# Sliding-window attention in halves of the TensorE array, with the softmax scaled on ScalarE

## The chip, the cores and the metric

The kernel runs on one core of one Trainium2 chip. The metric is the device time of one execution in microseconds (us). A core has TensorE (PE in the tables; PEld is its loading of weights), VectorE (DVE), ScalarE (ACT), GpSimd (POOL), and SyncE (SP), which issues most transfers. Each engine works through its own instructions in order; semaphores tie them together.

## The reference, cut to what matters

One decoder block on 256 tokens with model width 2048. Two attention branches run side by side and are merged by sigmoid gates; then follow an output projection, two RMSNorms and a gated feed-forward network with a short convolution. The change touches the attention of both branches:

```python
# MLA branch: 16 heads, query and key of 128 + 64, value of 128, causal
s = (einsum('bqhd,bkhd->bhqk', qn, k_nope) + einsum('bqhd,bkd->bhqk', qr, k_rope)) * scale
s = where(kpos[None, :] <= qpos[:, None], s, NEG)
p = softmax(s); o = einsum('bhqk,bkhd->bqhd', p, v)
# sliding branch: 32 heads of 64, 4 key/value heads, window 128, T5 bias, one sink per head
s = where(mask, einsum('bnqhgd,bnshd->bhgnqs', q, kb) * 0.125 + bias, NEG)
m = maximum(max(s), sink); e = exp(s - m)
p = e / (sum(e) + exp(sink - m)); o = einsum('bhgnqs,bnshd->bnqhgd', p, vb)
```

Everything is float32. The large products are made in three passes: each operand is split into a high part in the reduced format fp32r and a remainder in the same format, and high*high, high*low and low*high are summed.

## The kernel before, in words

The 1.5 ms are mostly weights that stream in, are split (`whi` by ScalarE on L116, `wlo` by VectorE on L117) and multiplied on TensorE (L129 to L131 and L137 to L139). The attention lies in the middle, from about 330 to 695 us. It is a loop over 8 pairs `i` (L593). In a pair, `pair_proj` makes the next pair's queries, keys and values; `step(2 * i)` and `step(2 * i + 1)` do the attention; `late_z` and, towards the end, the output projection give TensorE other matmuls. While they run, a background generator adds up modulation rows on VectorE (L235). A scheduler of the framework, working from its own estimates, sets the order of each engine's instructions at build time, so matmuls of the projections stand between those of the attention.

One `step(h)` handles one MLA head (index 0) and two sliding heads (1 and 2). Each has 256 queries as two blocks of 128; the first block sees 128 keys, the second 256, so a score matrix is 128 x 384. Its parts are:

- Scores (L520 to L530). Each head takes one PSUM bank of tag `sc`, of which there are two. For a sliding head the 64-row query is stacked: `stack` (L442 to L450) writes its high part into one half of the 128 rows and its remainder into the other half, and the keys `kss` hold the same 64 rows twice. One 128-row matmul thus gives high*k + low*k; two of them, for the keys' high and low part, make a block (L530).
- Mask, bias and row maximum on VectorE (L535), which frees the bank; then -max (L538), the sink (L540), exponentials with sums on ScalarE (L546) and 0.5/sum on VectorE (L548 to L550).
- Normalisation, six multiplications per step: `NORMS = "dpdpda"` gives the three 128-wide ones to VectorE, two 256-wide ones to GpSimd (both L558), and the last 256-wide one to ScalarE (L556).
- Three transposes per head on TensorE into a bank `tp` (L143 through L561), copied by ScalarE to `pT` (L563).
- Value products (L570, L571) into bank `o`: first the MLA head, with 128 output rows, then each sliding head with 64 output rows, head 1 in the lower and head 2 in the upper half. These operands are plain float32, and each such matmul shows up as two records in the trace.
- Gating (L573) and merging into `mix` (L576).

## Time and profile before

| | before |
|---|---|
| time, median of 3 runs | 1520.65 us (1518.46 to 1521.5) |
| time of the profiled execution | 1520.17 us |
| its span | 1518.3 us |
| PE busy | 1472.3 us (97%) |
| DVE busy | 1050.1 us (69%) |
| ACT busy | 754.4 us (50%) |
| POOL busy | 286.9 us (19%) |

The span runs from the first to the last instruction; some 2 us of the profiled time lie around it. A busy share is an average over stages, and the end of a matmul record is modelled: consecutive matmuls overlap, so what a matmul costs is read from the distance between starts, not from its duration.

### The profile page before, as it was taken

What the parts mean: (1) busy time and instruction counts of PE and PEld (TensorE: products, weight loads), DVE (VectorE), ACT (ScalarE), POOL (GpSimd) and SP (SyncE); (2) the same over time, 40 slices, a digit from 0 to 9 for tenths busy, and PEclk for the clock granted to TensorE, in tenths of its full rate; (3) what the DMA queues carried; (4) which work ended last, traced back from release to release, by engine and by line L of the source; (5) the groups of instructions that cost most, each with busy time, mean ns of one, the idle gap of its engine ahead of it and who ended that gap; (6) DMA issues with size and microseconds to landing.
All of it is one profiled execution on the core that took longest, in us unless ns stands there. A gap on an engine that the chain in (4) does not pass through costs nothing.

```text
span 1518.3 us, 27322 instructions
## 1 busy us (share of the span) xinstructions
PE 1472.3 (97%) x10914; PEld 1361.0 (90%) x10914; DVE 1050.1 (69%) x1384; ACT 754.4 (50%) x1165; POOL 286.9 (19%) x207
## 2 busy tenths in 40 slices
PE   7999999799999999999899999999999999999998
PEld 6988899789898898978799999999999999888886
DVE  3578868888787969777787777765666665444443
ACT  4534435545654655765564444554554454444342
POOL 0034215832525444320000010000000000000000
PEclk9999999999999999999999999999999999999999
DMA  9889868589587968669477788755556557666662
GB/s 371 295 313 328 308 234 262 178 264 306 175 306 240 298 197 274 197 208 358 183 250 259 254 277 266 225 181 183 182 181 190 182 181 242 191 193 192 194 193 99
DMA packets 101535, 357.14 MB, mean 235 GB/s; under 512 B 11760, under 2 KB 12208, under 8 KB 100896
## 3 DMA queue, kind: packets, MB, share of 16 engines
q1 hardware_dynamic: 99936, 350.82, 69.4%
q0 software_dynamic: 1472, 4.58, 1.2%
q8 instruction: 85, 1.39, 0.4%
q14 instruction: 42, 0.34, 0.1%
HBM read 351.11 MB, written 4.24 MB: 234 GB/s over the span
## 4 chain that ended last, share of the span: by engine, by line
PE 79%; DVE 9%; DMA 7%; issue 3%; ACT 1%; POOL 0%; DVEq 0%; SPq 0%; ACTq 0%; POOLq 0%
PE bk_mm L129 12%; PE bk_mm L131 12%; PE bk_mm L130 12%; PE bk_mm L137 4%; PE bk_mm L138 4%; PE bk_mm L139 4%; DMA raw<-in_w_ada_dram 4%; PE bk_sc L130 4%; PE bk_sc L129 4%; PE bk_sc L131 4%; PE bk_sc L138 3%; PE bk_sc L137 3%; PE bk_sc L139 3%; DVE wlo L117 3%; DVE acc L235 3%
## 5 line engine op out<-in xcount | busy, mean ns | idle before, releaser
L117 DVE TENSOR_TENSOR wlo<-raw,whi 128x1024 fp32r<-128x1024 f32 (+3 forms) x472 | 589.7, 1256 | 317.2 <-ACT whi L116 316.0
L116 ACT CAST whi<-raw 128x1024 fp32r<-128x1024 f32 (+3 forms) x472 | 478.1, 1019 | 531.7 <-PE bk_mm L130 161.6
L129 PE MATMUL bk_mm<-h_hi,whi 128*128 128x256 f32 x1824 | 522.6, 287 | 0.8 <-ACT h_hi L151 0.5
L131 PE MATMUL bk_mm<-h_hi,wlo 128*128 128x256 f32 x1824 | 518.0, 284 | 0.5 <-DVE wlo L117 0.5
L130 PE MATMUL bk_mm<-h_lo,whi 128*128 128x256 f32 x1824 | 518.4, 284 | 0.1
L129 PEld LDWEIGHTS bk_mm<-h_hi,whi 128*128 128x128 f32 x1824 | 350.9, 192 | 14.2 <-issue 8.7
L130 PEld LDWEIGHTS bk_mm<-h_lo,whi 128*128 128x128 f32 x1824 | 351.2, 193 | 1.1 <-issue 0.8
L131 PEld LDWEIGHTS bk_mm<-h_hi,wlo 128*128 128x128 f32 x1824 | 351.2, 193 | 1.2 <-DVE wlo L117 0.7
L235 DVE SCALAR_TENSOR_TENSOR acc<-raw,csil,acc 128x1024 f32<-128x1024 f32 (+1 forms) x141 | 188.6, 1337 | 58.2 <-DMA raw<-in_w_ada_dram 58.0
L129 PE MATMUL bk_sc<-h_hi,whi 128*128 128x256 f32 x560 | 158.7, 283 | 0.0
L130 PE MATMUL bk_sc<-h_lo,whi 128*128 128x256 f32 x560 | 158.6, 283 | 0.0
L131 PE MATMUL bk_sc<-h_hi,wlo 128*128 128x256 f32 x560 | 158.5, 283 | 0.0
L746 POOL TENSOR_TENSOR sa<-sa,u 128x512 f32<-128x512 f32 x22 | 32.7, 1486 | 469.1 <-DVE u L740 447.6
L129 PEld LDWEIGHTS bk_sc<-h_hi,whi 128*128 128x128 f32 x560 | 107.5, 192 | 0.4 <-ACT whi L116 0.4
L130 PEld LDWEIGHTS bk_sc<-h_lo,whi 128*128 128x128 f32 x560 | 107.5, 192 | 0.2 <-DVE h_lo L152 0.2
L131 PEld LDWEIGHTS bk_sc<-h_hi,wlo 128*128 128x128 f32 x560 | 107.5, 192 | 0.0
L363 POOL TENSOR_TENSOR pair<-pair,part 128x512 f32<-128x512 f32 x35 | 64.0, 1830 | 195.2 <-ACT part L362 195.1
L137 PE MATMUL bk_sc<-whi,g_hi 128*128 128x512 f32 x176 | 68.6, 390 | 0.0
L137 PE MATMUL bk_mm<-whi,g_hi 128*128 128x512 f32 x176 | 68.6, 390 | 0.0
L138 PE MATMUL bk_mm<-wlo,g_hi 128*128 128x512 f32 x176 | 68.5, 389 | 0.0
L139 PE MATMUL bk_mm<-whi,g_lo 128*128 128x512 f32 x176 | 68.5, 389 | 0.0
L138 PE MATMUL bk_sc<-wlo,g_hi 128*128 128x512 f32 x176 | 68.5, 389 | 0.0
(202 smaller groups left out, 2102.8 us busy)
## 6 DMA issues: line engine op xcount, KB each, us to landing
raw<-in_w_ada_dram SPq DMA_DIRECT2D x192, 512.0 KB, 5.0
raw<-in_w_up_dram SPq DMA_DIRECT2D x176, 512.0 KB, 4.3
raw<-in_w_in_dram SPq DMA_DIRECT2D x116, 512.0 KB, 5.1
raw<-in_w_down_dram SPq DMA_DIRECT2D x88, 512.0 KB, 4.4
raw<-in_w_o_dram SPq DMA_DIRECT2D x32, 512.0 KB, 5.0
raw<-in_w_uqn_dram SPq DMA_DIRECT2D x16, 384.0 KB, 4.1
bias<-trow POOLq DMA_DIRECT2D x16, 256.0 KB, 5.2
raw<-in_w_ukv_dram SPq DMA_DIRECT2D x16, 256.0 KB, 3.5
```

The source lines that it names most:

```text
L116: act.copy(hi[:, :n], raw[:, :n])
L117: dve.tensor_tensor(lo[:, :n], raw[:, :n], hi[:, :n].bitcast(F32), op=ALU.subtract)
L129: pe.matmul(o, wh, xh, start=start, stop=False)
L130: pe.matmul(o, wh, xl, start=False, stop=False)
L131: pe.matmul(o, wl, xh, start=False, stop=stop)
L137: pe.matmul(o, ch, wh, start=start, stop=False)
L138: pe.matmul(o, ch, wl, start=False, stop=False)
L139: pe.matmul(o, cl, wh, start=False, stop=stop)
L235: dve.scalar_tensor_tensor(acc[:, :w], r, csil[:, j:j + 1], acc[:, :w], op0=ALU.mult, op1=ALU.add)
L363: pool.tensor_tensor(pairs[i][:, :wd], pairs[i][:, :wd], part[:, :wd], op=ALU.add)
L746: pool.tensor_tensor(sa, sa, us[1], op=ALU.mult)
```

## The change

Three edits inside `step`, with a helper. First, the sliding heads' queries are no longer stacked: `split_pair2` keeps both heads in one tile, head 1 in rows 0 to 63 and head 2 in rows 64 to 127, with a tile for the high parts (`qsh`) and one for the remainders (`qsl`). The scores are 64-row matmuls, three per block and head (high*high, high*low, low*high), written head 1, head 2, head 1, ... so that neighbours use different row halves of the array and different banks. The sliding heads now come ahead of the MLA head. Second, all six normalisations go to ScalarE and `NORMS` disappears. Third, the value products come after all three heads' transposes, with three `pT` buffers in place of two: the two sliding heads alternate between the column halves, and the MLA head follows.

```diff
--- before.py
+++ after.py
@@ -30,7 +30,6 @@
 PUMP = 1.3
 RATES = (0.5, 0.8, 0.3, 0.5)
 SPREAD = 7.0
-NORMS = "dpdpda"
 SCT = (2, 4)
 NW1 = (5, 5, 5)
 NW2 = (4, 6, 6)
@@ -449,6 +448,14 @@
             pool.tensor_tensor(res[e][other], src[me], res[e][me].bitcast(F32), op=ALU.subtract)
         return res
 
+    def split_pair2(src):
+
+        hi = at.tile([P, 2 * T], F32R, tag="qsh", bufs=1, name="qsh")
+        lo = at.tile([P, 2 * T], F32R, tag="qsl", bufs=1, name="qsl")
+        act.copy(hi, src)
+        pool.tensor_tensor(lo, src, hi.bitcast(F32), op=ALU.subtract)
+        return hi, lo
+
     MLA_SCALE = 192.0 ** -0.5
     mixs = [None] * 8
     mx2 = []
@@ -505,8 +512,8 @@
         e = h % 2
         kv = h // 4
         if e == 0:
-            stacks[h // 2] = (stack(ropes[h // 2], "qr", T), stack(zt[h // 2][0], "qs", 2 * T))
-        qrs, qss = stacks[h // 2]
+            stacks[h // 2] = (stack(ropes[h // 2], "qr", T), split_pair2(zt[h // 2][0]))
+        qrs, qs = stacks[h // 2]
         zp = zt[h // 2]
         vst = pairs[7]
         bias = at.tile([P, 2, T], F32, tag="bias", name="bias")
@@ -517,30 +524,41 @@
 
         sm = at.tile([P, 3, 384], F32, tag="sm", bufs=2, name="sm")
         mx = at.tile([P, 6], F32, tag="mx", name="mx")
-        for i in range(3):
-            sc = bank("sc")
-            for c0, c1, q0, kw in ((0, P, 0, P), (P, 384, P, T)):
-                qsl = slice(e * T + q0, e * T + q0 + P)
-                if i == 0:
-                    pe.matmul(sc[:, c0:c1], qn[:, qsl], kn[:, e * T:e * T + kw], start=True, stop=False)
-                    for j in range(2):
-                        pe.matmul(sc[:, c0:c1], qrs[e][:, q0:q0 + P], krs[:, j, :kw], start=False, stop=j == 1)
-                else:
-                    for j in range(2):
-                        pe.matmul(sc[:, c0:c1], qss[i - 1][:, qsl], kss[:, j, kv, T - kw:], start=j == 0, stop=j == 1)
+        blocks = ((0, P, 0, P), (P, 384, P, T))
+
+        def masked(i, sc):
             for j, (c0, c1) in enumerate(((0, P), (P, 384))):
                 col = 2 * i + j
                 bt = cmask[:, P - c0:T] if i == 0 else bias[:, i - 1, :c1 - c0]
                 to = sm[:, i, c0:c1]
-                dve.tensor_tensor_reduce(to if i == 0 else down_order(to), sc[:, c0:c1], bt, 1.0, sink6[:, h, col:col + 1],
+                dve.tensor_tensor_reduce(to if i == 0 else down_order(to), sc[:, c0:c1], bt, 1.0,
+                                         sink6[:, h, col:col + 1],
                                          op0=ALU.add, op1=ALU.max, accum_out=mx[:, col:col + 1])
+
+
+        scs = [bank("sc") for _ in range(2)]
+        for c0, c1, q0, kw in blocks:
+            qsl = slice(e * T + q0, e * T + q0 + P)
+            for n, (qp, kp) in enumerate(((0, 0), (0, 1), (1, 0))):
+                for i in range(2):
+                    r = slice(64 * i, 64 * i + 64)
+                    pe.matmul(scs[i][:, c0:c1], qs[qp][r, qsl], kss[r, kp, kv, T - kw:], start=n == 0, stop=n == 2)
+        for i in range(2):
+            masked(i + 1, scs[i])
+        sc = bank("sc")
+        for c0, c1, q0, kw in blocks:
+            qsl = slice(e * T + q0, e * T + q0 + P)
+            pe.matmul(sc[:, c0:c1], qn[:, qsl], kn[:, e * T:e * T + kw], start=True, stop=False)
+            for j in range(2):
+                pe.matmul(sc[:, c0:c1], qrs[e][:, q0:q0 + P], krs[:, j, :kw], start=False, stop=j == 1)
+        masked(0, sc)
         nm = at.tile([P, 6], F32, tag="nm", name="nm")
         dve.tensor_scalar(nm, mx, -1.0, None, op0=ALU.mult)
         es = at.tile([P, 6], F32, tag="es", name="es")
         dve.tensor_tensor(es, sink6[:, h, :], nm, op=ALU.add)
         act.activation(es, es, AF.Exp)
         den = at.tile([P, 6], F32, tag="den", name="den")
-        for i in range(3):
+        for i in (1, 2, 0):
             for j, (c0, c1) in enumerate(((0, P), (P, 384))):
                 col = 2 * i + j
                 act.activation(sm[:, i, c0:c1], sm[:, i, c0:c1], AF.Exp, bias=nm[:, col:col + 1],
@@ -549,26 +567,23 @@
         dve.reciprocal(den, den)
         dve.tensor_scalar(den, den, 0.5, None, op0=ALU.mult)
         ob = bank("o")
-        for i in range(3):
+        pts = [None] * 3
+        for i in (1, 2, 0):
+            tp = bank("tp")
             for j, (c0, c1) in enumerate(((0, P), (P, 384))):
-                o, r = sm[:, i, c0:c1], den[:, 2 * i + j:2 * i + j + 1]
-                if NORMS[2 * i + j] == "a":
-                    act.mul(o, o, r)
-                else:
-                    (dve if NORMS[2 * i + j] == "d" else pool).tensor_scalar(o, o, r, None, op0=ALU.mult)
-            tp = bank("tp")
+                act.mul(sm[:, i, c0:c1], sm[:, i, c0:c1], den[:, 2 * i + j:2 * i + j + 1])
             for c in range(3):
                 turn_pe(tp[:, c * P:c * P + P], sm[:, i, c * P:c * P + P])
-            pT = at.tile([P, 384], F32, tag="pT", bufs=2, name="pT")
-            act.copy(pT, tp[:, :384])
-            if i == 0:
-                o = ob[:, 0:T]
-                vv = [vt[:, t * T + e * P:t * T + e * P + P] for t in range(2)]
-            else:
-                o = ob[64 * (i - 1):64 * i, T:2 * T]
-                vv = [vst[:, t * T + kv * 64:t * T + kv * 64 + 64] for t in range(2)]
-            pe.matmul(o, vv[0], pT[:, 0:T], start=True, stop=False)
-            pe.matmul(o[:, P:T], vv[1], pT[:, T:384], start=False, stop=True)
+            pts[i] = at.tile([P, 384], F32, tag="pT", bufs=3, name="pT")
+            act.copy(pts[i], tp[:, :384])
+
+        for t in range(2):
+            for i in (1, 2):
+                pe.matmul(ob[64 * (i - 1):64 * i, T + t * P:2 * T], vst[:, t * T + kv * 64:t * T + kv * 64 + 64],
+                          pts[i][:, t * T:T + t * P], start=t == 0, stop=t == 1)
+        for t in range(2):
+            pe.matmul(ob[:, t * P:T], vt[:, t * T + e * P:t * T + e * P + P], pts[0][:, t * T:T + t * P],
+                      start=t == 0, stop=t == 1)
         tm = at.tile([P, 512], F32, tag="tmp", name="tm")
         dve.scalar_tensor_tensor(tm, tg, 1.0, ob, op0=ALU.add, op1=ALU.mult)
         if e == 0:
```

The instructions move as follows; names carry buffer numbers, `bk_sc` is a score bank, `bk_o` the output bank, `bk_mm` and `bk_tp` the banks of other products and of transposes. Lines of the changed kernel are shifted: L545 are its sliding scores, L551 and L553 the MLA scores, L582 the sliding value products, L585 the MLA ones, L574 the normalisation, and L128 to L130, L142, L239 and L115 are L129 to L131, L143, L240 and L116 of before.

TensorE before, scores at the border of the third and fourth step:

```order
L530 MATMUL bk_sc_4519<-kss_2760,qs_4493 128x128 x2
L530 MATMUL bk_sc_4519<-kss_2760,qs_4493 128x256 x2
L525 MATMUL bk_sc_4581<-kn_3811,qn_3769 128x128
L527 MATMUL bk_sc_4581<-krs_2759,qr_4487 128x128 x2
L525 MATMUL bk_sc_4581<-kn_3811,qn_3769 128x256
L527 MATMUL bk_sc_4581<-krs_2759,qr_4487 128x256 x2
L129 MATMUL bk_mm_4653<-h_hi_243,whi_4656 128x256
```

TensorE of the changed kernel, sliding scores of the third step, the first of a pair (banks 4507 and 4508 are the two heads):

```order
L138 MATMUL bk_mm_4465<-whi_4458,blk_lo_3178 128x256
L545 MATMUL bk_sc_4507<-kss_2760,qsh_4498 128x128
L545 MATMUL bk_sc_4508<-kss_2760,qsh_4498 128x128
L545 MATMUL bk_sc_4507<-kss_2760,qsh_4498 128x128
L545 MATMUL bk_sc_4508<-kss_2760,qsh_4498 128x128
L545 MATMUL bk_sc_4507<-kss_2760,qsl_4499 128x128
L545 MATMUL bk_sc_4508<-kss_2760,qsl_4499 128x128
L545 MATMUL bk_sc_4507<-kss_2760,qsh_4498 128x256
L545 MATMUL bk_sc_4508<-kss_2760,qsh_4498 128x256
L545 MATMUL bk_sc_4507<-kss_2760,qsh_4498 128x256
L545 MATMUL bk_sc_4508<-kss_2760,qsh_4498 128x256
L545 MATMUL bk_sc_4507<-kss_2760,qsl_4499 128x256
```

And of the fourth step, the second of its pair, whose head 1 stands 25 projection matmuls earlier:

```order
L128 MATMUL bk_mm_4665<-h_hi_633,whi_4734 128x256
L545 MATMUL bk_sc_4590<-kss_2760,qsh_4498 128x128 x2
L545 MATMUL bk_sc_4590<-kss_2760,qsl_4499 128x128
L545 MATMUL bk_sc_4590<-kss_2760,qsh_4498 128x256 x2
L545 MATMUL bk_sc_4590<-kss_2760,qsl_4499 128x256
L551 MATMUL bk_sc_4607<-kn_3811,qn_3769 128x128
L553 MATMUL bk_sc_4607<-krs_2759,qr_4493 128x128 x2
L551 MATMUL bk_sc_4607<-kn_3811,qn_3769 128x256
L553 MATMUL bk_sc_4607<-krs_2759,qr_4493 128x256 x2
```

In the first step of a pair the heads alternate as written; in the second step the scheduler has taken them apart, and one head's six matmuls stand alone between other work.

TensorE, value products of the fourth step, before and then changed:

```order
L131 MATMUL bk_mm_4785<-h_hi_2574,wlo_4808 128x256
L570 MATMUL bk_o_4619<-pT_4626,vt_3854 128x256
L571 MATMUL bk_o_4619<-pT_4626,vt_3854 128x128
L570 MATMUL bk_o_4619<-pT_4636,pair_426 64x256
L571 MATMUL bk_o_4619<-pT_4636,pair_426 64x128
L240 MATMUL bk_tp_4792<-acc_3827,ones_87 32x256 x4
L129 MATMUL bk_mm_4785<-h_hi_2580,whi_4807 128x256
```

```order
L128 MATMUL bk_mm_4797<-h_hi_2580,whi_4886 128x256
L582 MATMUL bk_o_4631<-pT_4638,pair_426 64x256
L582 MATMUL bk_o_4631<-pT_4646,pair_426 64x256
L582 MATMUL bk_o_4631<-pT_4638,pair_426 64x128
L582 MATMUL bk_o_4631<-pT_4646,pair_426 64x128
L585 MATMUL bk_o_4631<-pT_4654,vt_3854 128x256
L585 MATMUL bk_o_4631<-pT_4654,vt_3854 128x128
L239 MATMUL bk_tp_4804<-acc_3827,ones_87 32x256 x4
```

Before, head 2's products follow later and by themselves; now both sliding heads stand together, ahead of the MLA head.

ScalarE around the normalisation of the first two steps, before and then changed:

```order
L541 ACTIVATE es<-es 128x6
L556 ACTIVATE sm<-sm,den 128x256
L116 CAST whi<-raw 128x768
L563 COPY pT<-bk_tp 128x384
L116 CAST whi<-raw 128x512
L563 COPY pT<-bk_tp 128x384
L556 ACTIVATE sm<-sm,den 128x256
L116 CAST whi<-raw 128x512
L563 COPY pT<-bk_tp 128x384 x2
```

```order
L574 ACTIVATE sm<-sm,den 128x256
L574 ACTIVATE sm<-sm,den 128x128
L574 ACTIVATE sm<-sm,den 128x256
L574 ACTIVATE sm<-sm,den 128x128
L574 ACTIVATE sm<-sm,den 128x256
L115 CAST whi<-raw 128x768
L578 COPY pT<-bk_tp 128x384
L115 CAST whi<-raw 128x768
L578 COPY pT<-bk_tp 128x384
```

Before, two multiplications stand among casts and copies; now twelve stand in a row (the last five are shown) ahead of the first copy.

## Rows read from the trace of the kernel before

**Rows 1.** The page: busy time and share of each engine; then the chain of work that ended last, by engine.

```profile
PE 1472.3 (97%) x10914; PEld 1361.0 (90%) x10914; DVE 1050.1 (69%) x1384; ACT 754.4 (50%) x1165; POOL 286.9 (19%) x207
...
PE 79%; DVE 9%; DMA 7%; issue 3%; ACT 1%; POOL 0%; DVEq 0%; SPq 0%; ACTq 0%; POOLq 0%
```

**Rows 2.** Busy time by stretch: start and end, length, busy us and instructions of PE, PEld, DVE, ACT and POOL, granted TensorE clock, DMA share, GB/s. The first is the whole attention, the others two short stretches in it.

```profile
330.00:695.00 365.00, 351.85 (x2578) 321.52 (x2578) 292.63 (x525) 209.34 (x461) 135.10 (x105) 0.99 0.75 245
...
337.00:343.00 6.00, 5.16 (x29) 5.09 (x30) 6.00 (x15) 2.41 (x4) 0.73 (x1) 0.72 0.89 316
601.00:606.00 5.00, 4.62 (x26) 4.48 (x27) 3.76 (x11) 2.13 (x4) 2.61 (x3) 0.66 0.91 292
```

**Rows 3.** What PE waited for from 330 to 700 us: total us, times, longest us.

```profile
PE bk_sc L530 <- DVE mx L535: 7.3, 5, 2.9
PE bk_tp L143 <- DVE sm L558: 5.0, 5, 2.1
PE bk_tp L143 <- POOL sm L558: 0.7, 2, 0.4
```

**Rows 4.** Timeline of PE around one sliding head's value product: start us, length us, instruction, records (start to start is the cost).

```profile
377.04 0.28 PE L129 MATMUL bk_mm<-blk_hi,whi 128*128 128x256 f32 x1
377.16 0.28 PE L130 MATMUL bk_mm<-blk_lo,whi 128*128 128x256 f32 x1
377.37 0.65 PE L570 MATMUL bk_o<-pT,pair 128*64 128x256 f32 x2
377.85 0.38 PE L571 MATMUL bk_o<-pT,pair 128*64 128x128 f32 x2
378.16 0.39 PE L131 MATMUL bk_mm<-blk_hi,wlo 128*128 128x256 f32 x1
378.39 0.28 PE L129 MATMUL bk_mm<-blk_hi,whi 128*128 128x256 f32 x1
378.50 0.28 PE L130 MATMUL bk_mm<-blk_lo,whi 128*128 128x256 f32 x1
```

**Rows 5.** The same view of an MLA head's value product, with 128 output rows.

```profile
616.57 0.28 PE L131 MATMUL bk_mm<-blk_hi,wlo 128*128 128x256 f32 x1
616.69 0.60 PE L570 MATMUL bk_o<-pT,vt 128*128 128x256 f32 x2
617.12 0.38 PE L571 MATMUL bk_o<-pT,vt 128*128 128x128 f32 x2
```

**Rows 6.** The same view of float32 products with 32 output rows: two of them (four records) on two quarters of the columns, and four of them (eight records) on all four quarters.

```profile
112.48 0.28 PE L131 MATMUL bk_mm<-h_hi,wlo 128*128 128x256 f32 x1
112.69 0.63 PE L227 MATMUL bk_sc<-raw,cpad 128*32 128x256 f32 x4
113.25 0.39 PE L137 MATMUL bk_mm<-whi,h_hi 128*128 128x256 f32 x1
...
157.98 0.28 PE L129 MATMUL bk_mm<-h_hi,whi 128*128 128x256 f32 x1
158.19 0.64 PE L240 MATMUL bk_sc<-acc,ones 128*32 128x256 f32 x8
158.76 0.38 PE L130 MATMUL bk_mm<-h_lo,whi 128*128 128x256 f32 x1
```

**Rows 7.** The same view of one sliding head's scores: two matmuls of 128 columns and two of 256 in one row.

```profile
625.56 0.28 PE L129 MATMUL bk_mm<-h_hi,whi 128*128 128x256 f32 x1
625.68 0.63 PE L530 MATMUL bk_sc<-kss,qs 128*128 128x128 f32 x4
626.14 0.29 PE L130 MATMUL bk_mm<-h_lo,whi 128*128 128x256 f32 x1
```

**Rows 8.** The same view of the one product of the program on fewer than 128 rows: 32 rows and 32 columns of the array, 384 columns streamed.

```profile
243.33 0.28 PE L131 MATMUL bk_mm<-h_hi,wlo 128*128 128x256 f32 x1
243.54 0.83 PE L318 MATMUL bk_tp<-oh,c_rel_bias 32*32 32x384 f32 x2
244.29 0.39 PE L129 MATMUL bk_mm<-h_hi,whi 128*128 128x256 f32 x1
244.52 0.28 PE L130 MATMUL bk_mm<-h_lo,whi 128*128 128x256 f32 x1
```

**Rows 9.** Groups by line and shape from 330 to 695 us (busy us, mean ns | idle before): the normalisations, and the exponentials of the same shapes.

```profile
L558 POOL TENSOR_SCALAR sm<-sm,den 128x256 f32<-128x256 f32 x32 | 43.2, 1358 | 44.6 <-DVE den L550 44.4
...
L546 ACT ACTIVATE sm<-sm,nm 128x128 f32<-128x128 f32 x48 | 18.8, 392 | 9.8 <-DVE nm L538 9.7
...
L558 DVE TENSOR_SCALAR sm<-sm,den 128x128 f32<-128x128 f32 x48 | 16.4, 405 | 0.2
...
L556 ACT ACTIVATE sm<-sm,den 128x256 f32<-128x256 f32 x16 | 8.1, 507 | 4.7 <-DVE den L550 4.6
```

**Rows 10.** Splitting the stacked queries (L448, L449), by line: number of each shape, ns min/median/max, first and last start. Then two groups of other lines with 128 rows of 512: busy us, mean ns | idle before.

```profile
L448 ACT CAST qs<-pair x16: 603/617/621, 265.0 to 629.2; 64x512 fp32r<-64x512 f32 x16
...
L449 POOL TENSOR_TENSOR qs<-pair,qs x16: 1286/1458/2302, 273.4 to 631.9; 64x512 fp32r<-64x512 f32 x16
...
L151 ACT CAST h_hi<-mix 128x512 fp32r<-128x512 f32 x8 | 4.8, 617 | 0.0
...
L746 POOL TENSOR_TENSOR sa<-sa,u 128x512 f32<-128x512 f32 x22 | 32.7, 1486 | 469.1 <-DVE u L740 447.6
```

**Rows 11.** The longest wait of ScalarE from 260 to 700 us: total us, times, longest us.

```profile
ACT whi L116 <- DMA raw<-in_w_in_dram: 43.2, 26, 3.7
```

## The prediction

> **What bounds the kernel now.** I read the page first: TensorE is busy 97% of the span, and 79% of the chain that ended last is its work [rows 1]. Then the table by stretch: in the 365 us of the attention TensorE is busy 351.85 us, VectorE 292.6, ScalarE 209.3, GpSimd 135.1 [rows 2]. Only 13.1 us are idle, and the list of waits names them: 7.3 us for a score bank that VectorE has not emptied, 5.0 and 0.7 us for transposes whose input VectorE or GpSimd has not normalised [rows 3]. Nothing there waits for weights. So the stage is as long as TensorE's own work plus these 13.1 us, and the timeline by starts tells what each matmul costs.
>
> **What it costs to leave the full array.** Between two projection matmuls lie 0.12 us (377.04 to 377.16), but the first 64-row product starts 0.21 after its forerunner, its two 256-column records take 0.48 together, the two of 128 columns 0.31, and the second projection matmul behind comes after 0.23 [rows 4]. An MLA product of the same shape needs 0.43 for the two 256-column records [rows 5], so half of that, 0.22, for the two of 128: 0.65 of pure work. From 377.16 to 378.39 are 1.23 us; less two steps of 0.12 that would be there anyway, the excursion costs 0.99, of which 0.34 are entering and leaving the mode. Two products on different column quarters take 0.56 us start to start and four take 0.57 [rows 6]: column parts do run at the same time.
>
> **Value products.** Before, 32 excursions of 0.99: 31.7 us. After, I counted the order: in 11 of 16 steps both heads stand together, one excursion of 0.65 + 0.34 = 0.99; in five steps other matmuls come between the first head's 256-column product and the rest, two excursions with 0.43 + 0.65 of work and 2 x 0.34 of mode: 1.76. Sum 10.9 + 8.8 = 19.7, a gain of 12.0 us. If halves did not overlap, the 11 steps would lose 0.65 each and the five 0.22: 8.2 back.
>
> **Scores.** Before, a sliding head's four matmuls take 0.46 us and change no mode [rows 7]: 32 x 0.46 = 14.7 us. That is 0.23 for one of 128 and one of 256 columns, so three products of a head are 3 x 0.23 = 0.69. After, in the first step of a pair the two heads alternate; if row halves overlap like column parts, that is 0.69 for both, 8 x 0.69 = 5.5. In the second step the heads stand apart, nothing overlaps, and 8 x 2 x 0.69 = 11.0. Then the mode: 12 excursions in the first steps (three of them are cut into pieces) and 16 in the second, 28 in all. The trace has no product on row halves. The nearest row is the one on 32 rows and 32 columns: the first start is 0.21 behind its forerunner, and the matmul after next follows after 0.23, as for 64 output rows [rows 8]. So I take 0.34 again, 9.5 us, with bounds of 0 (halving rows alone might need no change) and 0.45. The sum is 26.0, a loss of 11.3 us; with the bounds of the mode, 1.8 to 14.4.
>
> So the two halves of the change nearly cancel on TensorE: -12.0 + 11.3 = -0.7, and some 0.3 more for the pairs that are cut: -0.4. The MLA scores and products, and the transposes, are as many as before.
>
> A rule of the Trainium skill speaks against this sum: its page "TensorE: Matmul & The Clock Gate", Part 3 (Packing small matmuls), says that weight loads overlap matmuls in flight only where the row group differs, and the second steps use one row group six times running. This trace contradicts the rule for full-height matmuls, which share all row groups and still start 0.12 apart; for half-height ones no row shows it, so it is a rival below. The same section gives 3.07 times for four row tiles, not 4. By that ratio the alternating steps would cost some 0.90, not 0.69, an estimate of 1.7 us more.
>
> **Normalisation.** VectorE loses 48 instructions of 405 ns (16.4 us) and GpSimd 32 of 1358 (43.2); ScalarE gains 32 more of 507 ns (16.2) and 48 of 128 columns, for which the exponential of that shape, 392 ns, is the nearest row (18.8) [rows 9]. Splitting queries gives a little back: ScalarE casts 8 times instead of 16, at 617 ns, so 4.9 less, and GpSimd subtracts 8 times instead of 16 at 1458, 11.7 less [rows 10]; a tile of 128 rows takes as long as one of 64, as the 128x512 rows of other lines show, 617 and 1486 [rows 10]. ScalarE ends 30.1 us up, at 239 of 365 us; VectorE 16.4 down, at 276. None of this is on the path by itself: what counts is who waits.
>
> The waits for score banks, 7.3 us, come from VectorE's queue, and idle TensorE then runs at a lower clock for a while: the granted clock is 0.72 in 6 us around one such wait and 0.66 in 5 us after a wait for a transpose [rows 2]. At 1.2 GHz in place of 2.4 for 0.56 of 6 us and 0.68 of 5 us, each costs 1.7 us more. VectorE gets a twentieth of its work taken off and the sliding scores come earlier, before a pair's projections are done. I let the 7.3 + 1.7 = 9.0 us halve: -4.5, with bounds of 0 and -9.0. The waits for transposes, 5.7 + 1.7 = 7.4 us, I leave as they are: ScalarE takes over from two engines, and behind a multiplication that waits for its sum stand the casts of weights and the `pT` copies, whose absence TensorE would feel next. Twelve multiplications in a row, some 5.4 us, delay the first copy; TensorE has projection matmuls in between. If that cover is too short, the stall is new; if ScalarE is never late, the 7.4 us vanish.
>
> **Sum.** The profiled execution took 1520.17 us, 1.9 more than its span and 0.5 less than the median. 1520.2 - 0.4 - 4.5 = 1515.3 on that scale, 1515.8 against the median of 1520.65.
>
> **Rivals.**
> - Row halves need no change of mode. For it: the matmul streams the same 128 output columns as the full one. Against it: the 32-row product [rows 8], which also narrows the columns and so does not decide. It gives back 9.5: 1506.3.
> - Row halves hide no weight loads (slower). Mechanism and place: in the second steps the same half is loaded and used six times in a row. Price: a start that is not covered comes 0.10 late, as the matmul at 378.39 does (0.23 for 0.12) [rows 4]; 16 excursions of six, 9.6 us, and six pairs in each of eight alternating steps, 4.8; less 1.4 already in the mode cost, 13: 1528.8. It decides from about 0.06 us per matmul on. Against it: full-height matmuls do hide theirs.
> - ScalarE becomes what TensorE waits for (slower). For it: it already waits 43.2 us for weights from memory in these stages, with its queue blocked [rows 11], and the multiplications now stand in that queue. If half of the 16 steps wait as long as the longest now, 2.1 us [rows 3], that is 16.8 instead of 5.7: 1527.
> - Halves do not overlap at all, so the change does not do what it says: 8.2 from the values and 8 x 0.69 = 5.5 from the scores: 1529.5. Rows 6 speak against it for columns.
> - VectorE's relief shortens no wait, as the banks are asked for just as soon: 1520.2.
>
> **How the numbers follow.** Forecast 0.40, no mode change 0.15, weight loads 0.12, ScalarE 0.13, no overlap 0.05, no shorter wait 0.15. The range for 8 in 10 reaches from the free mode, 1506, to the slower rivals, 1529; the forecast's own is 1510 to 1521. A measurement of this kernel tells some 0.2%, 3 us, from no change: faster is below 1517.6, slower above 1523.7. Of the forecast I count two thirds as faster and nearly all the rest as no change; the free mode as faster; the last rival mostly as no change; the three others mostly as slower. This makes 0.46 faster, 0.29 no change, 0.25 slower.
>
> **What would show it.** In the timeline: two L582 of different heads some 0.01 us apart in their first record and about 1.0 us for the pair with its mode changes; two L545 of different banks likewise, and 0.7 us between the first and the last of twelve plus 0.34. If second steps show more than 0.12 between L545 starts, weight loads are not hidden; if the first L545 follows its forerunner after 0.12, the mode is free. In the list of waits, PE for the score bank should fall to some 3.7 us, and PE on ScalarE for L142 stay near 5.7; a sum of waits above 15 us, or PE's busy time in the attention off by more than 5 us, would make the forecast wrong.

## The result and the profile after

| | before | changed |
|---|---|---|
| median, us | 1520.49 (1518.46 to 1521.5, 4 runs) | 1528.47 (1526.01 to 1530.25, 4 runs) |
| ratio, 95% interval | | 1.0054 (1.0040 to 1.0067) |
| span of the profiled execution | 1518.3 | 1525.5 |

The changed kernel is slower by 8 us, 0.5%. I had forecast 1515.8, and called a time above 1523.7 slower. The page of the changed kernel, busy time and chain by engine, beside [rows 1]:

```profile
PE 1477.5 (97%) x10978; PEld 1365.7 (90%) x10978; DVE 1031.9 (68%) x1336; ACT 773.9 (51%) x1237; POOL 236.2 (15%) x167
...
PE 79%; DMA 9%; DVE 6%; issue 3%; ACT 2%; POOL 1%; DVEq 0%; SPq 0%; ACTq 0%; POOLq 0%
```

Nothing there tells where 8 us went. The table by stretch, columns as in [rows 2], tells more: the attention before, then the attention of the changed kernel and two short stretches in it.

```profile
330.00:700.00 370.00, 356.85 (x2601) 325.66 (x2601) 294.56 (x527) 211.75 (x467) 135.10 (x105) 0.99 0.76 248
```

```profile
330.00:700.00 370.00, 354.58 (x2614) 323.44 (x2613) 273.86 (x464) 228.84 (x532) 83.41 (x65) 0.97 0.74 240
386.00:395.00 9.00, 8.20 (x49) 7.49 (x49) 6.51 (x22) 3.36 (x14) 3.57 (x3) 0.81 0.84 251
581.00:592.00 11.00, 9.54 (x41) 8.91 (x42) 11.00 (x23) 3.46 (x4) 2.68 (x3) 0.53 0.85 265
```

TensorE idles 15.4 of 370 us, and 13.2 before. GpSimd lost 52 us of work and VectorE 21, as the edit meant them to, but the granted clock is 0.97 where it was 0.99: from 581 to 592 us it is 0.53, nearly all at 1.2 GHz in place of 2.4. What PE waited for from 330 to 700 us (columns as in [rows 3]):

```profile
PE bk_sc L551 <- DVE mx L534: 11.1, 4, 4.2
PE bk_mm L136 <- ACT qn L491: 2.1, 1, 2.1
PE bk_mm L128 <- ACT whi L115: 1.0, 1, 1.0
PE bk_o L582 <- DVE tm L588: 0.7, 1, 0.7
PE bk_mm L136 <- ACT whi L115: 0.5, 1, 0.5
```

The waits of transposes for a normalised input, 5.7 us before, are gone. The waits for a score bank rose from 7.3 to 11.1, in fewer and longer pieces. One of them in the timeline, TensorE and then VectorE (start, length, instruction):

```profile
578.12 0.28 PE L130 MATMUL bk_mm<-h_hi,wlo 128*128 128x256 f32 x1
582.46 0.80 PE L551 MATMUL bk_sc<-kn,qn 128*128 128x128 f32 x2 [4.06 <-DVE mx L534]
```

```profile
576.01 2.32 DVE L234 SCALAR_TENSOR_TENSOR acc<-raw,csil,acc 128x1024 f32<-128x1024 f32 x1
578.25 2.29 DVE L116 TENSOR_TENSOR wlo<-raw,whi 128x1024 fp32r<-128x1024 f32 x1
580.46 1.27 DVE L234 SCALAR_TENSOR_TENSOR acc<-raw,csil,acc 128x1024 f32<-128x1024 f32 x1
581.66 0.34 DVE L534 CUSTOM_DVE_ANT_0 sm<-bk_sc,bias,c_sink 128x128 f32<-128x128 f32 x1
581.93 0.47 DVE L534 CUSTOM_DVE_ANT_0 sm<-bk_sc,bias,c_sink 128x256 f32<-128x256 f32 x1
```

The MLA head's scores now come third and want the bank of the first sliding head. That head's scores were written from 572.2 us on; its mask takes 0.7 us, but stands in VectorE's queue behind two `acc` and a `wlo`. TensorE stands still for 4.06 us, and the low clock of the row 581 to 592 goes with it.

**One table for all runs.** To compare kernels I cut TensorE's time from 40 us to the first `sa<-u` (785.8 us before; what the change touches lies ahead of it) into three: gaps over 0.15 us, half of the busy time in stretches at 1.2 GHz (an estimate of what the low clock cost), and the rest, work at full clock. Kernels with the very same TensorE instructions gave 705.7 to 710.6 us of work, and rows_mla comes out 6 us below what its excursions add up to, so a work figure is good to some 6 us. These three are one execution's. The last column is not: the granted clock, as a share of the full one, is known for every execution, and (1 - clock) x span, averaged over all of a kernel's (4 of the changed kernel, 114 of before), is what the low clock cost in the whole span, good to 1 or 2 us.

| kernel | median, us | ratio to before (95%) | gaps | lost to low clock | work | low clock, all executions |
|---|---|---|---|---|---|---|
| before | 1520.5 | | 26.9 | 8.3 | 710.4 | 18.1 |
| changed | 1528.5 | 1.0054 (1.0040 to 1.0067) | 27.9 | 15.8 | 706.8 | 25.2 |
| v_only | 1518.8 | 0.9988 (0.9978 to 0.9999) | 30.4 | 10.0 | 703.4 | 18.1 |
| v21 | 1512.8 | 0.9956 (0.9940 to 0.9972) | 32.5 | 11.2 | 696.2 | 17.9 |
| s_only | 1532.6 | 1.0085 (1.0070 to 1.0101) | 28.1 | 14.0 | 716.9 | 20.4 |
| first_only | 1528.7 | 1.0050 (1.0032 to 1.0068) | 34.9 | 13.9 | 708.2 | 19.6 |
| rows_mla | 1528.6 | 1.0055 (1.0033 to 1.0077) | 20.7 | 9.2 | 723.7 | 13.7 |
| n_only | 1527.9 | 1.0053 (1.0035 to 1.0071) | 30.2 | 15.7 | 706.3 | 19.8 |
| n_dve | 1523.7 | 1.0025 (1.0012 to 1.0038) | 32.7 | 12.2 | 705.7 | 19.4 |
| n_pool | 1517.3 | 0.9987 (0.9974 to 0.9999) | 30.2 | 10.6 | 708.9 | 16.9 |
| act_dup | 1520.5 | 0.9994 (0.9980 to 1.0009) | 29.8 | 7.5 | 710.6 | 14.0 |
| after_stacked | 1515.9 | 0.9977 (0.9966 to 0.9989) | 31.9 | 16.3 | 695.0 | 20.8 |
| as_split | 1514.7 | 0.9962 (0.9950 to 0.9974) | 36.4 | 13.2 | 693.6 | 21.2 |
| as_split21 | 1511.6 | 0.9951 (0.9933 to 0.9968) | 34.6 | 12.3 | 692.6 | 19.5 |
| as_21 | 1514.4 | 0.9963 (0.9949 to 0.9977) | 36.5 | 17.0 | 692.1 | 20.7 |
| after_pool | 1518.6 | 0.9991 (0.9982 to 1.0000) | 27.7 | 10.3 | 706.5 | 19.7 |
| after_mlasc | 1524.2 | 1.0025 (1.0011 to 1.0040) | 27.3 | 12.0 | 709.6 | 20.3 |
| after_3sc | 1543.9 | 1.0152 (1.0130 to 1.0174) | 50.7 | 19.4 | 702.2 | 27.4 |
| best_mla | 1511.6 | 0.9943 (0.9927 to 0.9960) | 31.9 | 12.6 | 694.0 | 20.4 |
| best_dadada | 1514.9 | 0.9966 (0.9950 to 0.9981) | 36.0 | 13.2 | 694.8 | 19.4 |

The median of before was 1519.2 to 1520.1 in the later comparisons; differences to before in the text below are the ratio's, taken times 1520. Of the changed kernel's 7.2 us of span, 4.8 arise ahead of the first `sa<-u`: work -3.6, gaps +1.0, low clock +7.5. The other 2.4 come later; a stretch at 1.2 GHz near 967 us, which before has not, is worth 1.7 of them. Three other kernels show such a stretch, and I leave its cause open. The last column agrees on what the loss is: 7.1 us more low clock in the four executions, of 8 us in all.

### The profile page after: what moved, and what is told of

It is laid out like the page before. It is cut to its first block, busy times and chain, and to the rows that moved or that the text cites. A ratio compares the mean times of both kernels' runs of the same rounds, so it can differ in the third digit from the quotient of the medians.

```text
span 1525.5 us, 27386 instructions
## 1 busy us (share of the span) xinstructions
PE 1477.5 (97%) x10978; PEld 1365.7 (90%) x10978; DVE 1031.9 (68%) x1336; ACT 773.9 (51%) x1237; POOL 236.2 (15%) x167
## 4 chain that ended last, share of the span: by engine, by line
PE 79%; DMA 9%; DVE 6%; issue 3%; ACT 2%; POOL 1%; DVEq 0%; SPq 0%; ACTq 0%; POOLq 0%
PE bk_mm L128 13%; PE bk_mm L130 12%; PE bk_mm L129 12%; DMA raw<-in_w_ada_dram 5%; PE bk_mm L136 4%; PE bk_mm L137 4%; PE bk_mm L138 4%; PE bk_sc L128 4%; PE bk_sc L129 4%; PE bk_sc L130 4%; PE bk_sc L138 3%; PE bk_sc L136 3%; PE bk_sc L137 3%; DVE wlo L116 2%; DMA raw<-in_w_in_dram 2%
## 5 line engine op out<-in xcount | busy, mean ns | idle before, releaser
L116 DVE TENSOR_TENSOR wlo<-raw,whi 128x1024 fp32r<-128x1024 f32 (+3 forms) x472 | 586.7, 1251 | 317.5 <-ACT whi L115 310.5
L115 ACT CAST whi<-raw 128x1024 fp32r<-128x1024 f32 (+3 forms) x472 | 477.4, 1019 | 518.4 <-PE bk_mm L129 148.9
L128 PE MATMUL bk_mm<-h_hi,whi 128*128 128x256 f32 x1824 | 524.8, 288 | 1.9 <-ACT whi L115 1.0
L130 PE MATMUL bk_mm<-h_hi,wlo 128*128 128x256 f32 x1824 | 519.9, 286 | 0.0
L129 PE MATMUL bk_mm<-h_lo,whi 128*128 128x256 f32 x1824 | 519.7, 285 | 0.0
L128 PEld LDWEIGHTS bk_mm<-h_hi,whi 128*128 128x128 f32 x1824 | 352.0, 193 | 16.6 <-issue 9.7
L129 PEld LDWEIGHTS bk_mm<-h_lo,whi 128*128 128x128 f32 x1824 | 352.1, 193 | 2.0 <-issue 1.6
L130 PEld LDWEIGHTS bk_mm<-h_hi,wlo 128*128 128x128 f32 x1824 | 351.8, 193 | 1.0 <-issue 0.2
L234 DVE SCALAR_TENSOR_TENSOR acc<-raw,csil,acc 128x1024 f32<-128x1024 f32 (+1 forms) x141 | 192.2, 1363 | 71.2 <-DMA raw<-in_w_ada_dram 70.8
L128 PE MATMUL bk_sc<-h_hi,whi 128*128 128x256 f32 x560 | 159.1, 284 | 0.0
L129 PE MATMUL bk_sc<-h_lo,whi 128*128 128x256 f32 x560 | 158.7, 283 | 0.0
L130 PE MATMUL bk_sc<-h_hi,wlo 128*128 128x256 f32 x560 | 158.7, 283 | 0.0
L128 PEld LDWEIGHTS bk_sc<-h_hi,whi 128*128 128x128 f32 x560 | 107.9, 193 | 0.4 <-issue 0.4
L129 PEld LDWEIGHTS bk_sc<-h_lo,whi 128*128 128x128 f32 x560 | 107.8, 192 | 0.0
L130 PEld LDWEIGHTS bk_sc<-h_hi,wlo 128*128 128x128 f32 x560 | 107.8, 192 | 0.0
L761 POOL TENSOR_TENSOR sa<-sa,u 128x512 f32<-128x512 f32 x22 | 32.5, 1479 | 472.0 <-DVE u L755 453.8
```

Source lines behind the costliest of these rows:

```text
L115: act.copy(hi[:, :n], raw[:, :n])
L116: dve.tensor_tensor(lo[:, :n], raw[:, :n], hi[:, :n].bitcast(F32), op=ALU.subtract)
L128: pe.matmul(o, wh, xh, start=start, stop=False)
L129: pe.matmul(o, wh, xl, start=False, stop=False)
L130: pe.matmul(o, wl, xh, start=False, stop=stop)
L234: dve.scalar_tensor_tensor(acc[:, :w], r, csil[:, j:j + 1], acc[:, :w], op0=ALU.mult, op1=ALU.add)
```

## The experiments

### The value products alone

```diff
+        pts = [None] * 3        # all three transposes first
...
+        for t in range(2):
+            for i in (1, 2):    # v21: (2, 1)
...
```

v_only: 

> The kernel before with one part of the change: the value products stand together after the last transpose, the two sliding heads' on column halves in turn; scores and normalisation as before. Both theories put TensorE's work 12.0 us lower (32 excursions into another mode of 0.99 us become 16 cheaper ones), so about 1508.5 us, a ratio of 0.992. Theory W (the work terms of the prediction hold, and the loss of the change came from longer waits for score banks and the slower clock behind them): the banks' order is that of before, so the waits for the masks stay near 7 us and the time falls by nearly the whole 12 us, 1507 to 1512. Theory R (the row halves cost much more than the 11.3 us I put on them, and the waits are a side show): the same here. A time above 1516 would say that the value term itself was wrong.

v21: 

> The kernel before with only its value products moved together, the second sliding head's written first; its order now cuts none of the 16 excursions, where the first such kernel, with the heads written the other way, cut 15. Work by the price list: 16 x 0.99 = 15.8 us against 31.7, so 15.9 us less. Theory B (what eats savings is the bank order with the sliding heads' scores first; here the MLA head's come first as before): waits for the masks stay near 7 us and nearly all of it shows, 1502 to 1506. Theory P (VectorE's work and the loads behind it pace this stretch too, so that work saved on TensorE mostly turns into waits and slow clock, wherever they fall): TensorE's idle time between 250 and 785 us grows from 27 us to 32 or more, 1508 to 1514.

v_only is 1.8 us faster, not 12. I had assumed that heads written together stay together; its trace shows that the scheduler put the first head's first product ahead of the second head's transposes in 15 of 16 steps, two excursions each. 15 x 1.76 + 0.99 = 27.4 us, 4.3 less than before, and TensorE's time in value products fell by 3.8 us. With the later head written first none is cut: 12.5 us less in value products, 14.2 less work. Time in value products is counted from start to start and takes in the MLA head's. The price list holds; but 15.9 us were expected and 6.7 came. Gaps grew by 5.6, as theory P has it, though the banks are asked for in the old order. The low clock, 2.9 us more in this trace, is no more than before's over all executions (17.9 and 18.1).

### The scores alone

```diff
# s_only: split_pair2, row halves and MLA scores last, as changed
# rows_mla: s_only with the MLA head's scores first
# first_only: before, with
-        for i in range(3):
+        for i in (1, 2, 0):
             sc = bank("sc")
```

s_only: 

> The kernel before with the other part: sliding heads' scores on the row halves, first, and the MLA head's behind them; value products and normalisation as before. Theory W: work 11.3 + 0.3 us up, and the two banks taken at once bring the longer waits of the changed kernel too (4 us more, with 7 us more of slow clock), so 1532 to 1544, and the waits for the masks near 11 us, not 7. Theory R (row halves alone cost about 20 us): 1540, with the waits as before, near 7 us, and no more slow clock than before.

first_only: 

> The kernel before with only the order of a step's stacked scores changed, the two sliding heads' ahead of the MLA head's: the same instructions on every engine. Theory B2 (that order alone makes the longer waits of the third bank, 10 to 13 us against 7.3): 4 us of waits and some slow clock more, 1524 to 1530. Theory O: 1514 to 1526, no sign foretold.

rows_mla: 

> The kernel before with the sliding heads' scores on row halves but the MLA head's scores left first, so without the new order of scores that cost 7.6 us by itself. Nearly every lone head's six matmuls are an excursion of their own (32 in all): 32 x 0.39 = 12.5 us by the price list. If the price list holds and order is apart: 1530 to 1534. If the 12.5 us of the run with both (rows and sliding heads first) were mostly the order's, with 7.6 of them, rows cost 4 to 6 us and this is 1523 to 1527.

s_only's 12.9 us look like the term of the prediction, but they are a mixture. first_only issues the same instructions as before and loses 7.6 us; the scheduler makes a new order of it on every engine. Its attention, and its two largest waits from 330 to 700 us, of which the first is that of the MLA scores, now third in a step:

```profile
330.00:700.00 370.00, 347.96 (x2532) 319.54 (x2531) 286.78 (x510) 207.22 (x456) 139.79 (x102) 0.97 0.72 238
```

```profile
PE bk_sc L525 <- DVE mx L535: 9.8, 4, 4.1
PE bk_mm L137 <- ACT qn L484: 3.9, 1, 3.9
```

In all, first_only waits 12.1 us for score banks there, 4.8 more than before, and its gaps in the table are 8.0 us longer. The low clock is 1.5 us more over all executions, so most of its loss is waiting.

rows_mla has the rows without that order: 13.3 us more work in the table. The 12.5 of its expectation are the mode's price alone (0.39 a head, measured below) and leave out the third matmul of a block. With it a lone head takes 0.69 + 0.39 = 1.08 us, and the list gives 32 x (1.08 - 0.46) = 19.8; in its trace most lone heads take 1.07 or 1.08 us. The time is only 8.4 us up, and the waits shrink:

```profile
330.00:700.00 370.00, 364.81 (x2632) 329.52 (x2631) 285.18 (x523) 201.93 (x447) 127.53 (x98) 0.99 0.72 238
```

```profile
PE bk_sc L553 <- DVE mx L535: 1.9, 3, 1.0
PE bk_sc L542 <- DVE mx L535: 1.7, 1, 1.7
```

The waits for score banks are 3.6 us, half of before's 7.3, which fits a TensorE that comes later for them. So each lone head costs in work what the list says, and the order of the scores costs by itself. Whether the two add is not shown: 8.4 + 7.6 is 3.1 more than s_only's 12.9, but s_only's heads overlap in part and cost some 6 us less by the list.

### The normalisation alone

```diff
-NORMS = "dpdpda"
+NORMS = "aaaaaa"      # n_only;  n_dve "apapaa";  n_pool "dadada"
...
+                if NORMS[2 * i + j] != "a":          # act_dup, NORMS as before
+                    act.mul(dup[:, c0:c1], cmask[:, P - c0:T], r)
```

n_only: 

> The kernel before with all six normalisations of a step on ScalarE and nothing else. Theory W and theory R: ScalarE is 51% busy, nothing changes beyond 2 us: 1518.5 to 1522.5. Rival S (ScalarE's added 80 to 90 instructions put off what TensorE waits for): the loss of the change is here, 1526 to 1530, with more TensorE waits released by ScalarE.

n_dve: 

> The kernel before with only VectorE's three normalisations of a step moved to ScalarE (48 of 96 in all; GpSimd keeps its two). Theory L (ScalarE's added load itself costs, by putting off casts and copies that others wait for): half to two thirds of the 8 us, 1523 to 1526. Theory O (the new order decides: each placing of the same work lands its gaps and slow stretches differently, up to some 8 us either way): no fixed relation to the 8 us, anywhere in 1516 to 1528.

n_pool: 

> The kernel before with only GpSimd's two normalisations of a step moved to ScalarE (32 in all; VectorE keeps its three). Theory L: a third of the 8 us, 1522 to 1524. If GpSimd's slow normalisations of 1.36 us were what TensorE waits for: 1516 to 1519. Theory O: anywhere in 1516 to 1528.

act_dup: 

> The kernel before with its normalisation left where it is, and ScalarE given the same 80 scalings again beside it, on a constant tile and into a tile that nothing reads (about 32 us of ScalarE). Theory L: the load alone brings the 8 us, 1526 to 1530. Theory O: the time follows the gaps; if TensorE's order of instructions stays that of before, 1518 to 1522.

n_only costs 8.1 us, as rival S said, but act_dup gives ScalarE the same load and costs nothing:

```profile
330.00:700.00 370.00, 355.30 (x2599) 323.66 (x2598) 290.70 (x527) 236.17 (x543) 138.32 (x105) 1.00 0.76 246
```

ScalarE is 236.17 us busy there, more than in the changed kernel, and the granted clock is 1.00. So, in that kernel, it isn't ScalarE's load. n_dve and n_pool, +3.8 and -2.0, differ in sign. The trace of n_only has more stretches at 1.2 GHz (15.7 us lost against 8.3), but over its six executions the low clock costs only 1.7 us more than before, so most of its loss is something else; its gaps are 3.3 us longer. Its order on every engine is a new one; which moved instruction makes the loss, these runs don't tell.

### Parts taken back from the changed kernel

```diff
# after_stacked: the changed kernel with
-        scs = [bank("sc") for _ in range(2)]
...
+        for i in (1, 2, 0):
+            sc = bank("sc")
...
# as_split: after_stacked with NORMS = "dpdpda" back; as_split21: and
-            for i in (1, 2):
+            for i in (2, 1):
# as_21: after_stacked with (2, 1);  after_pool: the changed kernel with NORMS back
```

after_stacked: 

> The changed kernel with the sliding heads' scores taken back to stacked full-row products, still ahead of the MLA head's; value products and normalisation as changed. Theory W: TensorE's work falls by 12 us from the changed kernel's, and since one bank at a time is asked for, the waits for masks fall from 11 us towards 7 and the slow stretches go from 27 us towards 14: 1507 to 1513. Theory R: 1508, all from the row halves' work, with the waits still near 11 us. The waits and the granted clock of the trace tell the two apart, not the time alone.

as_split: 

> Stacked scores with the sliding heads first and value products together, as in the run before, but the normalisation shared among the three engines as in the kernel before. Its order keeps 15 of 16 steps' sliding value products in one excursion and cuts one: 15 x 0.99 + 1.76 = 16.6 us against 31.7, so work is 15.1 us below the kernel before. Theory N (putting all normalisations on ScalarE costs about 8 us by itself, as it did alone, through more and longer gaps and slow clock behind them): that cost is gone, 1505, range 1502 to 1508, and the slow stretches of the trace near 20 us in all. Rival C (the 8 us belonged to that kernel's order by chance, and every new order pays about as much): 1513, with 30 us or more of slow stretches.

as_split21: 

> As the run before it, with the second sliding head's value product written ahead of the first's; its order cuts no excursion: 16 x 0.99 = 15.8 us, work 15.9 us below the kernel before. Theory N: 1504, range 1501 to 1508. Rival C: 1512.

after_pool: 

> The changed kernel with only the normalisation taken back to three engines; scores on row halves, value products together (15 whole excursions, 1 cut: 3.1 us less work than the changed kernel's 11 and 5). Theory N: 1528.2 - 3.1 - 8 = 1517, range 1513 to 1521. Rival C, and the theory that row halves' work is the whole loss: only the 3.1 us go, 1525.

as_21: 

> Stacked scores, normalisation all on ScalarE, value products with the second sliding head's first: its order cuts none of the 16 excursions where the same kernel with the other order cut 6, so 6 x 0.77 = 4.6 us less work than its 1515.9. Theory N: 1511, range 1508 to 1515. Rival C: anything from 1505 to 1518, set by its gaps.

Without row halves the changed kernel is 11.7 us faster and beats before by 3.5: the rows' work (11.8 less) is worth its price there. Theory W's second half fell: the waits for masks did not shrink (9.9 + 2.7 us from 330 to 700), as theory R has it. The low clock cost as much as in the changed kernel in this trace (16.3 us), but 4.4 us less over all executions. Taking the normalisation back gave the changed kernel 9.6 us (3.1 from value excursions), as theory N said; with stacked scores it gave only 2.3 (as_split, whose value excursions alone should give 3.9) and 1.8 (as_split21 against as_21), as rival C said. So the price of the normalisation isn't a constant either. In the traces of all four pairs (n_only and before, changed and after_pool, after_stacked and as_split, as_21 and as_split21) having it on ScalarE lost 3.1 to 7.4 us more to low clock, but over all executions the differences are 1.7, 5.5, -0.4 and 1.2: only that of the changed kernel is clear.

### Relief for the banks

```diff
# after_mlasc: the changed kernel, MLA scores ahead of the sliding heads'
# after_3sc: the changed kernel with
-    PSN = {"mm": 3, "sc": 2, "tp": 2, "o": 1}
+    PSN = {"mm": 2, "sc": 3, "tp": 2, "o": 1}
```

after_mlasc: 

> The changed kernel with the MLA head's scores ahead of the two sliding heads' (one edit). Its order has all 32 score excursions of six matmuls in one piece (the lone heads in turn, none of twelve), which by the price list is 32 x 0.39 = 12.5 us on the rows against 11 to 12 before, and 15 of 16 value excursions whole (3.1 us less). Theory B: waits for masks fall from 11 to 7 us and slow stretches from 41 to near 27 us in all: 1515 to 1521. Theory N or P: only the value excursions' 3 us, 1524 to 1527.

after_3sc: 

> The changed kernel with three banks for scores and two, not three, for the projections. Theory B: the wait of the third bank of each step (11.1 us) goes, and with it most of the slow stretches behind it, so 1516 to 1522, if the projections do with two banks. Theory P: the wait moves to the projections' banks and the time is the same or longer, 1526 to 1535.

```profile
PE bk_sc L552 <- DVE mx L534: 6.8, 6, 2.1
```

after_mlasc gains 4.4 us, though its work grows. Its expectation counted the mode alone: all 32 heads stand alone, 32 x 1.08 = 34.6 us by the list, where the changed kernel's heads overlap in the first steps and cost 27.4; the value excursions give 3.1 back, so work is some 4 us up (2.8 in the table). Against that the waits for score banks (L552 are its sliding scores) are 6.8 us, no more than before's, as theory B has it, and the low clock is 4.9 us down over all executions; gaps hardly fell. The time itself is at the edge of theory N and P's range. So the order of the scores costs some 4 us or more in the changed kernel too. after_3sc is the slowest of all: its waits for score banks fall to 5.6 us, but the projections, with two banks, take the waits over (50.7 us of gaps), as theory P has it and worse.

### A kernel that beats both

```diff
# best_mla: v21 with, in exponentials, normalisation and transposes,
-        for i in range(3):
+        for i in (1, 2, 0):
# best_dadada: and NORMS = "dadada"
```

best_mla: 

> Stacked scores with the MLA head's first as before; normalisation on three engines; sliding heads' transposes first and their value products together, second head first: 16 whole excursions, 15.9 us less work. It differs from the run at 1511.6 only in which scores come first. Theory B: the waits for masks fall from 12 + 2 us to about 7, the wait for the sliding keys (3.5) goes, and with half of the slow stretches' excess the time is 1502 to 1506. Theory P: the order of the scores only moves the gaps, 1509 to 1514.

best_dadada: 

> The fastest kernel so far (stacked scores with the MLA head's first, value products together, 1511.6) with GpSimd's two normalisations of a step moved to ScalarE, which alone was worth 2.6 us on the kernel before. If gains of this kind add: 1509. Theory O: within 4 us of 1511.6 on either side.

```profile
330.00:700.00 370.00, 351.31 (x2638) 327.28 (x2638) 295.64 (x531) 215.19 (x472) 134.30 (x105) 0.98 0.77 252
```

```profile
PE bk_sc L530 <- DVE mx L535: 10.7, 6, 4.5
PE bk_tp L143 <- DVE sm L560: 5.4, 3, 3.7
```

At 1511.6 us best_mla is 8.7 us below before and 17 below the changed kernel. as_split21, which differs from it only in the order of the scores, has the same median, so here that order costs nothing that can be measured. Theory B fell: with the old order of scores the waits for banks are 10.7 us all the same. best_dadada lost 3.5 where the same edit had gained 2.0. One set of kernels shows how 16.4 us of saved work give only 8.7: those with the MLA scores first and `NORMS` as before. In order of work, 723.7 (rows_mla), 710.4 (before), 703.4 (v_only), 696.2 (v21), 694.0 (best_mla), gaps and low clock together are 29.9, 35.2, 40.4, 43.7 and 44.5 us: 14.6 us more for 29.7 us less work. In this set half of the work saved is given back. It is no rule: with the sliding heads first, as_split21 has 15.6 us less work than first_only and is 15.0 us faster, and after_stacked has 11.8 less than the changed kernel and is 11.7 faster.

## Why the prediction was wrong

- **Value products, -12.0: right, to 2 us.** TensorE's time in them, the MLA head's with it, fell by 10.3 us, from 36.9 to 26.6. One excursion with both heads, and the MLA head behind:

```profile
416.33 0.28 PE L128 MATMUL bk_mm<-h_hi,whi 128*128 128x256 f32 x1
416.54 0.87 PE L582 MATMUL bk_o<-pT,pair 128*64 128x256 f32 x8
417.34 0.92 PE L585 MATMUL bk_o<-pT,vt 128*128 128x256 f32 x4
```

Four products of two heads take 0.80 us start to start, entry apart; one head's two took 0.79 (377.37 to 378.16) [rows 4]. The halves overlap fully.

- **Scores, +11.3: right.** With the mode at the 0.39 measured below, the sum is 27.4 in place of 26.0, a loss of 12.7. Work is 11.8 us lower in after_stacked than in the changed kernel, 12.9 lower in as_split than in after_pool and 8.7 lower in first_only than in s_only, each good to some 6 us. Twelve matmuls of two heads, then a lone head's six:

```profile
378.11 0.28 PE L138 MATMUL bk_mm<-whi,blk_lo 128*128 128x256 f32 x1
378.32 0.44 PE L545 MATMUL bk_sc<-kss,qsh 64*128 64x128 f32 x4
...
379.20 0.39 PE L128 MATMUL bk_mm<-h_hi,whi 128*128 128x256 f32 x1
379.43 0.28 PE L129 MATMUL bk_mm<-h_lo,whi 128*128 128x256 f32 x1
```

```profile
592.79 0.28 PE L128 MATMUL bk_mm<-h_hi,whi 128*128 128x256 f32 x1
593.00 0.43 PE L545 MATMUL bk_sc<-kss,qsh 64*128 64x128 f32 x2
593.28 0.27 PE L545 MATMUL bk_sc<-kss,qsl 64*128 64x128 f32 x1
593.39 0.45 PE L545 MATMUL bk_sc<-kss,qsh 64*128 64x256 f32 x2
...
593.88 0.39 PE L129 MATMUL bk_mm<-h_lo,whi 128*128 128x256 f32 x1
594.11 0.28 PE L130 MATMUL bk_mm<-h_hi,wlo 128*128 128x256 f32 x1
```

Both take 1.32 us from the forerunner to the second matmul behind; less 2 x 0.12 and 0.69 of work, the mode costs 0.39 (I took 0.34). The free mode, the missing overlap and the uncovered weight loads fall with it: six matmuls on one row half are no slower than twelve on both, and 593.28 to 593.39 is 0.11. The rule of the Trainium skill, page "TensorE: Matmul & The Clock Gate", Part 3, that a weight load overlaps a matmul in flight only where row groups differ, doesn't hold in this trace.

- **"I let the 7.3 + 1.7 = 9.0 us halve: -4.5" is the step that failed.** The bank waits rose by 3.8, to 11.1 us, and the low clock cost 7.1 us more over all executions, 7.5 in the trace: that alone is nearly the whole loss. In the trace, stretches at 1.2 GHz that go with three bank waits (they end at 335.86, 386.80 and 582.46) took 7.9 us, where the one such stretch before took 1.7. My bounds for the term, 0 to -9.0, had no loss in them, and neither had the rival that the relief shortens no wait. I argued from totals, that VectorE has a twentieth less to do. But the timeline at 578 us shows a wait set by what stands ahead of a mask in VectorE's queue when TensorE wants that bank, and putting the sliding scores first changed that. This order costs 7.6 us without anything else (first_only), and taking it out of the changed kernel brings the bank waits back to 6.8 us (after_mlasc). It has no fixed price: best_mla and as_split21 don't differ. I had the new order in hand and counted excursions in it, but not the distance from each mask to the bank's next use, nor the `wlo` and `acc` ahead of it.

- **The normalisation, "None of this is on the path by itself": wrong too.** Taking the move to ScalarE back gives the changed kernel 9.6 us, 3.1 of them from value excursions (after_pool), so some 6.5 us are its own, while the bank waits stay near 10. The rival that named ScalarE was near in time, but its mechanism, eight waits of 2.1 us, is not what happened: waits for ScalarE are 3.6 us from 330 to 700 us, in three pieces. Stretches at 1.2 GHz after two of them, at 431 and 513 us, took another 3.4. ScalarE's busy time rose by 17 us, not 30, since multiplications in a row overlap: twelve took 4.26 us from 350.51 on, where I had put 5.4. act_dup shows that the load is free in the kernel before. Which moved instruction costs, and why only some 2 us come back where the scores are stacked, stays open.

- **Transposes' waits, "I leave as they are": wrong, to the good.** 5.7 us went to none. It didn't pay, for the gaps came up elsewhere, 1.0 us more in all.

- **"So the stage is as long as TensorE's own work plus these 13.1 us": too simple.** Gaps are not a constant to be added. TensorE meets VectorE's and ScalarE's queues every step, and of work saved between nothing and more than half came back as waits and low clock. My own sign of being wrong, a sum of waits above 15 us, came true by a little, at 15.4. And the forecast's -0.4 of work (-3.6 measured, within the error of that figure) could not tell the sign.

- **Three parts, one loss.** Taking back any one of them (after_pool, after_stacked, after_mlasc) takes 4.4 to 5.5 us of low clock off. No one part explains the changed kernel by itself.

## What to carry to other kernels

Price an edit's work from start-to-start distances; here that held to a few us. But on an engine 97% busy that meets in-order queues, expect that some of a saving may come back as waits (here from nothing to more than half), and give the term for waits a loss as well as a gain. Where a scheduler sets the order, look at the order itself before counting on instructions that are written together (v_only, v21), and run the order of the change without the change (first_only): here it alone was worth 7.6 us. Test a suspected load by doubling it where nothing depends on it (act_dup). And take the low clock from all executions, not from one trace: n_only's trace alone would have named the wrong cause.

## What was not expected of the hardware

Entering and leaving the row-half mode costs nearly the same as the column-half mode, 0.39 and 0.34 us, so a lone sliding head's scores on half of the rows take 1.08 us where the full rows took 0.46, though the halves do run side by side. A gap of 4.06 us on TensorE went with a granted clock of 0.53 over 11 us, so the wait cost about twice its length: half of the 9.54 us that TensorE was busy there, nearly all at 1.2 GHz, is over 4 us more. The price is not fixed: the gap of 4.21 us that ended at 386.80 went with 0.81 over 9 us, 1.7 us more.
